# A softmax's reciprocal as a power on GpSimd, and its maximum on VectorE, in a two-layer encoder on one core

## Chip, cores, metric

One core of one Trainium2 chip. The metric is device time in microseconds of one execution of the whole program, median of the runs. Lower is better.

## What is computed

An encoder of two layers on 512 tokens of width 1024, all in float32. The first layer's attention has two groups of eight heads (grouped-query with normalised, rotated queries and keys; and latent attention with a shared rotary key). The second layer's is a neighbourhood attention of 16 heads. Each layer ends in a squared-ReLU MLP, and a last RMSNorm follows. Cut to what the change touches:

```python
def block_attention(q, k, v, scale):          # first layer, 16 heads
    sc = jnp.einsum('bkgqd,bksd->bkgqs', qblk, kt).astype(jnp.float32) * scale
    p = jax.nn.softmax(sc, axis=-1).astype(vt.dtype)
    return jnp.einsum('bkgqs,bksd->bkgqd', p, vt)

def neighbourhood_attention(h, w_qkv, rpb, w_out):   # second layer, 16 heads
    sc = jnp.einsum('bhqd,bhqkd->bhqk', qblk, kg).astype(jnp.float32) * scale + bias[None]
    p = jax.nn.softmax(sc, axis=-1).astype(vg.dtype)
    return jnp.einsum('bhqk,bhqkd->bhqd', p, vg)
```

A softmax row is exp(x - max), divided by its own sum. The division is done as a multiplication by the reciprocal of the sum.

## The kernel before

Every matmul operand is split into a high and a low part (two float32r tiles), and a product takes three matmuls: high by high, high by low, low by high. TensorE (PE) does these and all transposes. ScalarE (ACT) rounds the high parts, makes exponentials and copies PSUM banks out; VectorE (DVE) subtracts to get the low parts, adds results, and does row statistics; GpSimd (POOL) does some additions and subtractions of weights and the multiplications by the reciprocals. SyncE (SP) issues nearly all DMAs.

**First attention** (`attend`, lines 958 to 1029). The 16 heads are taken one after the other, each in four blocks of 128 queries, so there are 64 score tiles of 128x512. `scores` makes one: two or three matmuls (L997) into one of two PSUM banks `s`; a custom DVE instruction (L1001) that scales the scores by a negative number from the table `scA` or `scB`, writes them to a tile `p` in SBUF and leaves each row's minimum in `t[:, 1:2]`; ACT's exponential of minus that tile with the minimum as its bias (L1003), which leaves the row sum in `t[:, 2:3]`; DVE's reciprocal (L1004); POOL's multiplication of the 128x512 tile by it (L1005). Three blocks later, `transpose` turns the tile by four PE transposes (L972) into a bank `t`, ACT and DVE split it (L974, L975), and after every second block `values` multiplies by the head's values (L985, eight matmuls) and `fold` adds the parts (L946, L949). Between blocks PE is given other matmuls, "fill": the projections that later heads need and the first half of the output projection (L501 to L503, L907 to L909), 1.5 us by the kernel's own account after each block. There are two banks each of `s` and `t`, three of `mm`, one of `o`, and five tiles `p`. The order of instructions on each engine is here not the code's: a scheduler of the framework sets it when the program is built. On POOL stand also, in this stage, rotary multiplications (L562, L563), sums of squares (L705) and low parts of weights (L202).

**Second attention** (`attend_C`, lines 1409 to 1530). Here the code's order is kept on PE, ACT, DVE and POOL (`fixed_order`). A head has four units of 128 queries by 256 keys. `scores` makes two units (L1426) and their minimum with the bias added (L1441); `weigh` makes the exponentials (L1460); `norm` the reciprocal on DVE (L1429) and the multiplication on POOL (L1430); `turn` transposes the previous head's units (L1452). So a product of `norm` is read a head later.

**The MLPs** take most of the rest. Their weights are summed on POOL (L302 to L304), then split by ACT and DVE (L308, L309); the change does not touch them.

Of the kernel before, what the change touches and what calls it, by code (L numbers as in the profile page):

```python
# [8 lines left out]
F32 = mybir.dt.float32  # L9
F32R = mybir.dt.float32r  # L10
I32 = mybir.dt.int32
AF = mybir.ActivationFunctionType
ALU = mybir.AluOpType
AX = mybir.AxisListType
PSUM = bass.MemoryType.PSUM

S = 512
D = 1024
P = 128
# [11 lines left out]
def f32(ap):  # L31
    return ap.bitcast(F32)
# [3 lines left out]
def encoder_kernel(ctx: ExitStack, tc: tile.TileContext, ins, out, dbg=None):  # L36
    nc = tc.nc
    PE, ACT, DVE, POOL, SP = nc.tensor, nc.scalar, nc.vector, nc.gpsimd, nc.sync
# [22 lines left out]
    def nm(s):  # L61
        cnt[0] += 1
        return f"{s}_{cnt[0]}"
# [18 lines left out]
    def sbk():  # L82
        return bank("s", 2)

    def stb():
        return bank("t", 2)

    def ob():
        return bank("o", 1)
# [4 lines left out]
    def tiny(n, dt=F32):  # L94
        return tp.tile([P, n], dt, tag=f"ti{n}", name=nm("ti"))

    def keep(shape, dt, name):
        return big.tile(shape, dt, tag=name, name=name)
# [8 lines left out]
    POOL.memset(ones, 1.0)  # L107
    zeros = keep([P, 1], F32, "zeros")
    POOL.memset(zeros, 0.0)
    gs = Slot(F32)  # L110
    ACT.dma_start(cst, ins["cst"][:, 0:C_ROPE])
    ACT.dma_start(gs.t[0:16, 0:P], ins["norm_mix"].rearrange("l (k p) -> (l k) p", p=P))
# [358 lines left out]
    class Fill:  # L471
# [8 lines left out]
        def step(self):  # L480
            try:
                self.credit -= next(self.q[0][1])
            except StopIteration:
                self.q.pop(0)
# [42 lines left out]
    def bcast_cols(col_ap, nparts, bk):  # L527

        for i in range(4):
            PE.transpose(bk[0:nparts, i * P : (i + 1) * P], col_ap(i), ident)  # L530
# [38 lines left out]
    def stats_to_tok(bk, n, name):  # L569

        st = scratch()
        ACT.activation(st[0:n, :], bk[0:n, :], AF.Copy)
        tb = stb()
        for i in range(4):
            PE.transpose(tb[:, i * n : (i + 1) * n], st[0:n, i * P : (i + 1) * P], ident[0:n, 0:n])
        v = keep([P, 4 * n], F32, name)
        v3 = v.rearrange("p (i n) -> p i n", i=4)
        DVE.tensor_tensor(v3, tb[:, 0 : 4 * n].rearrange("p (i n) -> p i n", i=4),
                          r0sq.unsqueeze(2).to_broadcast([P, 4, n]), op=ALU.mult)
        DVE.tensor_scalar(v, v, 1.0, EPS, op0=ALU.mult, op1=ALU.add)  # L580
        y = rsqrt(v, 4 * n)
        DVE.tensor_tensor(v3, y.rearrange("p (i n) -> p i n", i=4),
                          r0.unsqueeze(2).to_broadcast([P, 4, n]), op=ALU.mult)
        return v3
# [17 lines left out]
    def ind2(t):  # L602
        return cst[:, C_I2 + 2 * t : C_I2 + 2 * t + 2]
# [103 lines left out]
    def q_scales():  # L707
        rs = stats_to_tok(hold["stq"], 8, "rsQ")
        sc = keep([P, 4, 8], F32, "scA")
        DVE.tensor_scalar(sc, rs, -0.125, 1.0, op0=ALU.mult, op1=ALU.mult)  # L710
        hold["scA"] = sc


# [93 lines left out]
    def latents():  # L807

        b = stb()
        for z in range(2):  # L810
            PE.matmul(b[0:2, :], ind2(z), sqs[z].t[:, 0:512], start=z == 0, stop=z == 1)
        sB = stats_to_tok(b, 2, "rsB")
        for z in range(2):
            sqs[z].free()
        scB = keep([P, 4], F32, "scB")
        DVE.tensor_scalar(scB, sB[:, :, 0], -(96.0 ** -0.5), 1.0, op0=ALU.mult, op1=ALU.mult)
        bk = stb()
        bcast_cols(lambda i: sB[:, i, 1:2].to_broadcast([P, P]), P, bk)
        hold["skvb"] = Slot(F32)
        ACT.activation(hold["skvb"].t[:, 0:512], bk, AF.Copy)  # L820
        hold["sB"], hold["scB"] = sB, scB
        for s_ in X:
            s_.free()
        yield 1.5
# [136 lines left out]
    def attend(heads, step):  # L961


        late_t, late_v = [], []

        def transpose(h, i, p):
            if i % 2 == 0:
                h["pt"] = Slot(), Slot()
            h3, l3 = (s_.t.rearrange("p (k q) -> p k q", k=4)[:, :, (i % 2) * P : (i % 2 + 1) * P] for s_ in h["pt"])
            tb = stb()  # L970
            for k in range(4):
                PE.transpose(tb[:, k * P : (k + 1) * P], p[:, k * P : (k + 1) * P], ident)  # L972
            t3 = tb.rearrange("p (k q) -> p k q", k=4)
            ACT.activation(h3, t3, AF.Copy)  # L974
            DVE.tensor_tensor(l3, t3, f32(h3), op=ALU.subtract)  # L975
            if i % 2:
                late_v.append((h, i // 2, h["pt"]))

        def values(h, half, pt):
            if half == 0:  # L980
                h["o"] = ob()
            o = h["o"]
            for k in range(4):
                for n, m in enumerate(pt):
                    PE.matmul(o[:, 256 * half : 256 * half + 256], h["vlhs"](k), m.t[:, 256 * k : 256 * k + 256],  # L985
                              start=k == 0 and n == 0, stop=k == 3 and n == 1, skip_group_check=True)
            for s_ in pt:
                s_.free()
            if half:
                fold(o, h["e"])  # L990
                h["after"]()

        def scores(h, i):
            s = sbk()
            pl = h["passes"](i)
            for n, (lh, rh) in enumerate(pl):
                PE.matmul(s, lh, rh, start=n == 0, stop=n == len(pl) - 1)  # L997
            h["done"](i)
            t = tiny(4)
            p = pp.tile([P, 512], F32, tag="p", name=nm("p"))  # L1000
            DVE.tensor_tensor_reduce(p, s, zeros.to_broadcast([P, S]), op0=ALU.add, op1=ALU.min, scale=h["scale"](i),  # L1001
                                     scalar=3e38, accum_out=t[:, 1:2])
            ACT.activation(p, p, AF.Exp, bias=t[:, 1:2], scale=-1.0, accum_out=t[:, 2:3])  # L1003
            DVE.reciprocal(t[:, 3:4], t[:, 2:3])  # L1004
            POOL.tensor_scalar(p, p, t[:, 3:4], 1.0, op0=ALU.mult, op1=ALU.mult)  # L1005
            return p

        for h in heads:
            for i in range(4):
                ripe = list(late_v)  # L1010
                p = scores(h, i)
                if len(late_t) == 3:
                    transpose(*late_t.pop(0))
                late_t.append((h, i, p))
                if ripe:
                    values(*late_v.pop(0))
                step(h, i)
        for x in late_t:
            transpose(*x)
            while late_v:  # L1020
                values(*late_v.pop(0))
            fill.run(1.5)
# [389 lines left out]
    def attend_C(step):  # L1412
# [13 lines left out]
                PE.matmul(s, lh, rh[n], start=first and n == 0, stop=n == 1, skip_group_check=True)  # L1426

        def norm(p, tt):
            DVE.reciprocal(tt[:, 2:3], tt[:, 1:2])  # L1429
            POOL.tensor_scalar(p, p, tt[:, 2:3], 1.0, op0=ALU.mult, op1=ALU.mult)  # L1430

        def scores(h, us):
# [63 lines left out]
        for n in range(16):  # L1496
            t, e = n // 2, n % 2
# [4 lines left out]
            h = dict(d=PC[t], e=e, n=n)  # L1502
# [226 lines left out]
```

## Time and profile before

| | |
|---|---|
| runs, us | 1185.4, 1184.7, 1183.35; median 1184.7 |
| span of the profiled execution, first to last instruction | 1184.0 us |
| mean granted TensorE clock | 0.994 |
| PE busy | 1160.5 us, 98% |
| DVE, ACT, POOL busy | 883.2, 640.3, 526.1 us |
| first exponential of the first attention starts | 74.6 us |
| last one | 243.1 us |
| second attention, first and last multiplication on POOL | 641.8 and 808.1 us |

The page gives the profiled execution's span and no other time for it; it is 0.7 us under the median of the runs. Times in the trace count from the span's start. In a row of instructions the first two numbers are start and length in us; in brackets stands how long the engine sat idle before it and what released it. In a group's row, "x64 | 46.2, 724 | 92.3" means 64 instructions, 46.2 us busy in all, 724 ns mean, and 92.3 us of idle time of that engine just ahead of them. A row of waits reads "engine, tile and line, <- who was waited for: us in total, times, longest". Ends of matmuls are modelled and overlap, so PE's pace is read from start to start.

### The profile page before, as it was taken

To read this page: it belongs to the slowest core of one execution; us is meant where nothing else is said; L and a number is where in the kernel's file an instruction comes from. 1 tells how busy PE (TensorE), PEld (TensorE's weight loads), DVE (VectorE), ACT (ScalarE), POOL (GpSimd) and SP (SyncE) were. 2 spreads that over 40 slices of the span, in tenths; PEclk is the share of its full clock that TensorE was granted. 3 is DMA by queue.
4 is the path that set the end of the run, shared out by engine and by line. 5 is a ranking of instruction groups with operands and counts; after the bars stand their busy time and mean duration, and the time that the engine had idled before them with its cause. 6 is when DMAs were issued, how large, how long until landed. Compare 5 with 4: busy or idle time off the path is not lost.

```text
span 1184.0 us, 19784 instructions
## 1 busy us (share of the span) xinstructions
PE 1160.5 (98%) x7128; PEld 1021.2 (86%) x7128; DVE 883.2 (75%) x1514; ACT 640.3 (54%) x1081; POOL 526.1 (44%) x662
## 2 busy tenths in 40 slices
PE   9989999999999999999999999999999999999997
PEld 8667778888899899988998998988889989998895
DVE  5788998878967368786884676667996736778975
ACT  4468676664546247562553565555554624666344
POOL 3267343224562377819602232231376625774710
PEclk9999999999999999999999999999999999999998
DMA  7223225212524723225226464433352341322412
GB/s 244 71 54 92 68 78 134 62 56 77 167 86 134 263 70 90 72 90 165 67 72 178 131 184 126 116 112 109 107 165 76 115 134 55 98 64 89 143 36 71
DMA packets 110145, 128.01 MB, mean 108 GB/s; under 512 B 9075, under 2 KB 86816, under 8 KB 110048
## 3 DMA queue, kind: packets, MB, share of 16 engines
q1 hardware_dynamic: 106992, 119.30, 33.5%
q0 software_dynamic: 2304, 6.31, 2.2%
q8 instruction: 56, 0.92, 0.3%
q10 hardware_dynamic: 752, 1.15, 0.3%
q14 instruction: 41, 0.34, 0.1%
HBM read 104.32 MB, written 6.29 MB: 93 GB/s over the span
## 4 chain that ended last, share of the span: by engine, by line
PE 81%; DVE 4%; ACT 1%; issue 1%; POOL 0%; DVEq 0%; ACTq 0%
PE mm L503 8%; PE mm L501 8%; PE mm L502 8%; PE mm L390 4%; PE mm L389 4%; PE mm L388 4%; PE t L388 3%; PE t L389 3%; PE t L390 3%; PE s L502 2%; PE s L503 2%; PE s L501 2%; PE s L390 2%; PE s L388 2%; PE s L389 2%; PE s L997 2%
## 5 line engine op out<-in xcount | busy, mean ns | idle before, releaser
L309 DVE TENSOR_TENSOR wlo<-a,whi 128x896 fp32r<-128x896 f32 x132 | 161.8, 1230 | 83.7 <-ACT whi L308 82.9
L308 ACT ACTIVATE whi<-a 128x896 fp32r<-128x896 f32 x132 | 125.0, 950 | 155.0 <-PE o L502 45.8
L501 PE MATMUL mm<-a,whi 128*128 128x512 f32 x485 | 195.9, 406 | 0.9 <-DVE a L915 0.7
L503 PE MATMUL mm<-a,wlo 128*128 128x512 f32 x485 | 192.1, 397 | 2.5 <-DVE wlo L202 2.5
L502 PE MATMUL mm<-a,whi 128*128 128x512 f32 x485 | 192.5, 397 | 0.1
L202 DVE TENSOR_TENSOR wlo<-raw,whi 128x1024 fp32r<-128x1024 f32 (+4 forms) x117 | 139.3, 1193 | 66.4 <-ACT whi L212 63.9
L212 ACT ACTIVATE whi<-raw 128x1024 fp32r<-128x1024 f32 (+3 forms) x120 | 116.4, 971 | 92.2 <-PE s L502 39.8
L302 POOL TENSOR_TENSOR a<-a 128x128 f32<-128x128 f32 x132 | 85.1, 645 | 173.3 <-DMA a<-in_ffn_w_up_dram 103.9
L303 POOL TENSOR_TENSOR a<-a 128x256 f32<-128x256 f32 x132 | 120.2, 910 | 10.3
L304 POOL TENSOR_TENSOR a<-a 128x128 f32<-128x128 f32 x132 | 115.1, 872 | 10.3
L503 PEld LDWEIGHTS mm<-a,wlo 128*128 128x128 f32 x485 | 91.7, 189 | 23.7 <-DVE wlo L202 3.4
L501 PEld LDWEIGHTS mm<-a,whi 128*128 128x128 f32 x485 | 91.8, 189 | 20.4 <-PE t L972 0.9
L502 PEld LDWEIGHTS mm<-a,whi 128*128 128x128 f32 x485 | 91.9, 190 | 17.4 <-DVE a L545 0.4
L388 PE MATMUL mm<-a,whi 128*128 128x256 f32 x370 | 103.9, 281 | 0.0
L389 PE MATMUL mm<-a,whi 128*128 128x256 f32 x370 | 103.9, 281 | 0.0
L390 PE MATMUL mm<-a,wlo 128*128 128x256 f32 x370 | 103.7, 280 | 0.0
L1005 POOL TENSOR_SCALAR p<-p,ti 128x512 f32<-128x512 f32 x64 | 46.2, 724 | 92.3 <-DVE ti L1004 81.1
L1430 POOL TENSOR_SCALAR p<-p,ti 128x256 f32<-128x256 f32 x64 | 35.6, 567 | 104.8 <-DVE ti L1429 91.8
L388 PE MATMUL t<-a,whi 128*128 128x256 f32 x264 | 74.2, 281 | 0.0
L389 PE MATMUL t<-a,whi 128*128 128x256 f32 x264 | 74.1, 281 | 0.0
L390 PE MATMUL t<-a,wlo 128*128 128x256 f32 x264 | 73.9, 280 | 0.0
L390 PEld LDWEIGHTS mm<-a,wlo 128*128 128x128 f32 x370 | 69.6, 188 | 0.2 <-DVE wlo L309 0.2
(338 smaller groups left out, 3210.8 us busy)
## 6 DMA issues: line engine op xcount, KB each, us to landing
a<-in_ffn_w_up_dram SPq DMA_DIRECT2D x104, 256.0 KB
raw<-in_ffn_w_down_dram SPq DMA_DIRECT2D x46, 512.0 KB
raw<-in_od_w_qkv_dram SPq DMA_DIRECT2D x64, 128.0 KB
a<-in_ffn_w_down_dram SPq DMA_DIRECT2D x28, 256.0 KB
raw<-in_ffn_w_up_dram SPq DMA_DIRECT2D x12, 512.0 KB
raw<-in_ev_w_in_dram SPq DMA_DIRECT2D x12, 384.0 KB
a<-a SPq DMA_DIRECT2D x18, 256.0 KB
bias<-bx SPq DMA_DIRECT2D x16, 256.0 KB
```

Source lines behind the costliest of these rows:

```text
L202: z = lambda: (eng or DVE).tensor_tensor(to, src, f32(high), op=ALU.subtract)
L212: ACT.activation(hi[:, 0:m], raw[:, 0:m], AF.Copy)
L303: POOL.tensor_tensor(r[:, 4:6], r[:, 2:3].to_broadcast([P, 2, P]), r[:, 0:7:6], op=ALU.add)
L304: POOL.tensor_tensor(r[:, 7], r[:, 3], r[:, 5], op=ALU.subtract)
L308: ACT.activation(hi[:, 0:896], raw[:, 128:1024], AF.Copy)
L309: DVE.tensor_tensor(lo[:, 0:896], raw[:, 128:1024], f32(hi[:, 0:896]), op=ALU.subtract)
L388: PE.matmul(o, wh, x[:, 0], start=kp == 0 and n in (0, 1, 3, 5), stop=False, skip_group_check=True)
L389: PE.matmul(o, wh, x[:, 1], start=False, stop=False, skip_group_check=True)
L390: PE.matmul(o, wl, x[:, 0], start=False, stop=kp == self.np - 1, skip_group_check=True)
L501: PE.matmul(o, wh, xh, start=first, stop=False)
L502: PE.matmul(o, wh, xl, start=False, stop=False)
L503: PE.matmul(o, wl, xh, start=False, stop=last)
```

## The change

In the first attention DVE now takes the row's maximum straight from the score bank and writes no tile. POOL multiplies the maximum by the scale and by -1. ACT reads the scores from the bank, scales them (the tables `scA` and `scB` become positive), adds the bias, and writes the tile `p`. POOL raises the row sum to the power -1, with a constant column `minus`, ahead of its multiplication. In the second attention only the reciprocal is replaced in the same way. After the first hunk all line numbers are higher by two: L1004 of the new kernel is the scaling, L1006 the power, L1007 the multiplication, L999 the scores, L974 the transposes, L987 the values, L503 to L505 the fill.

```diff
@@ -107,6 +107,8 @@
     zeros = keep([P, 1], F32, "zeros")
     POOL.memset(zeros, 0.0)
+    minus = keep([P, 1], F32, "minus")
+    POOL.memset(minus, -1.0)
@@ -707,7 +709,7 @@
-        DVE.tensor_scalar(sc, rs, -0.125, 1.0, op0=ALU.mult, op1=ALU.mult)
+        DVE.tensor_scalar(sc, rs, 0.125, 1.0, op0=ALU.mult, op1=ALU.mult)
@@ -813,7 +815,7 @@
-        DVE.tensor_scalar(scB, sB[:, :, 0], -(96.0 ** -0.5), 1.0, op0=ALU.mult, op1=ALU.mult)
+        DVE.tensor_scalar(scB, sB[:, :, 0], 96.0 ** -0.5, 1.0, op0=ALU.mult, op1=ALU.mult)
@@ -998,10 +1000,10 @@
             h["done"](i)
             t = tiny(4)
             p = pp.tile([P, 512], F32, tag="p", name=nm("p"))
-            DVE.tensor_tensor_reduce(p, s, zeros.to_broadcast([P, S]), op0=ALU.add, op1=ALU.min, scale=h["scale"](i),
-                                     scalar=3e38, accum_out=t[:, 1:2])
-            ACT.activation(p, p, AF.Exp, bias=t[:, 1:2], scale=-1.0, accum_out=t[:, 2:3])
-            DVE.reciprocal(t[:, 3:4], t[:, 2:3])
+            DVE.tensor_reduce(t[:, 0:1], s, axis=AX.X, op=ALU.max)
+            POOL.tensor_scalar(t[:, 1:2], t[:, 0:1], h["scale"](i), -1.0, op0=ALU.mult, op1=ALU.mult)
+            ACT.activation(p, s, AF.Exp, bias=t[:, 1:2], scale=h["scale"](i), accum_out=t[:, 2:3])
+            POOL.tensor_tensor(t[:, 3:4], t[:, 2:3], minus, op=ALU.pow)
             POOL.tensor_scalar(p, p, t[:, 3:4], 1.0, op0=ALU.mult, op1=ALU.mult)
             return p
@@ -1426,7 +1428,7 @@
         def norm(p, tt):
-            DVE.reciprocal(tt[:, 2:3], tt[:, 1:2])
+            POOL.tensor_tensor(tt[:, 2:3], tt[:, 1:2], minus, op=ALU.pow)
             POOL.tensor_scalar(p, p, tt[:, 2:3], 1.0, op0=ALU.mult, op1=ALU.mult)
```

Since the scheduler orders the first attention, the change moves more than it edits. POOL, at the start of the second group of eight heads, before (`ti` is the small tile `t` of the code, `p` the 128x512 tile; the numbers tell tiles apart, and the first of the two is the same in both kernels):

```order
L1005 TENSOR_SCALAR p_409_1788<-p_409_1788,ti_408_1787 128x512
L1005 TENSOR_SCALAR p_413_1805<-p_413_1805,ti_412_1804 128x512
L1005 TENSOR_SCALAR p_420_1833<-p_420_1833,ti_419_1832 128x512
L202 TENSOR_TENSOR wlo_444_1902<-raw_435_1885,whi_443_1901 128x2x256
L202 TENSOR_TENSOR wlo_444_1902<-raw_435_1885,whi_443_1901 128x2x128
L1005 TENSOR_SCALAR p_424_1850<-p_424_1850,ti_423_1849 128x512
```

The same engine and place in the changed kernel:

```order
L1004 TENSOR_SCALAR ti_408_1821<-ti_408_1821,scB_1415 128x1
L1004 TENSOR_SCALAR ti_412_1839<-ti_412_1839,scB_1415 128x1
L1006 TENSOR_TENSOR ti_408_1821<-ti_408_1821,minus_82 128x1
L1007 TENSOR_SCALAR p_409_1822<-p_409_1822,ti_408_1821 128x512
L1006 TENSOR_TENSOR ti_412_1839<-ti_412_1839,minus_82 128x1
L1007 TENSOR_SCALAR p_413_1840<-p_413_1840,ti_412_1839 128x512
L1004 TENSOR_SCALAR ti_419_1868<-ti_419_1868,scB_1415 128x1
L1006 TENSOR_TENSOR ti_419_1868<-ti_419_1868,minus_82 128x1
L1007 TENSOR_SCALAR p_420_1869<-p_420_1869,ti_419_1868 128x512
L1004 TENSOR_SCALAR ti_423_1886<-ti_423_1886,scB_1415 128x1
L1006 TENSOR_TENSOR ti_423_1886<-ti_423_1886,minus_82 128x1
L1007 TENSOR_SCALAR p_424_1887<-p_424_1887,ti_423_1886 128x512
```

One row a tile became three, and but for a few pairs as the first one here the scaling of a tile stands behind the multiplication of the tile ahead of it; that goes on so through the stage, with the other POOL work of the stage between.

TensorE at the score tile that comes right after these four (number 36 of 64, counted from 0), before (`s` the score banks, `t` the transposes, `mm` the fill's banks):

```order
L997 MATMUL s_445_1916<-a_368_1605,a_350_1529 128x512 x3
L972 MATMUL t_448_1926<-cst_75,p_413_1805 128x128 x4
L501 MATMUL mm_430_1878<-a_293_1302,whi_439_1893 128x512
L502 MATMUL mm_430_1878<-a_293_1302,whi_439_1893 128x512
L503 MATMUL mm_430_1878<-a_293_1302,wlo_440_1894 128x512
L501 MATMUL mm_431_1879<-a_293_1302,whi_439_1893 128x512
L502 MATMUL mm_431_1879<-a_293_1302,whi_439_1893 128x512
L503 MATMUL mm_431_1879<-a_293_1302,wlo_440_1894 128x512
L997 MATMUL s_449_1939<-a_368_1605,a_350_1529 128x512 x3
L972 MATMUL t_454_1951<-cst_75,p_420_1833 128x128 x4
```

The same tiles in the changed kernel:

```order
L999 MATMUL s_445_1954<-a_368_1634,a_350_1556 128x512 x3
L974 MATMUL t_448_1965<-cst_75,p_413_1840 128x128 x4
L999 MATMUL s_449_1978<-a_368_1634,a_350_1556 128x512 x3
L974 MATMUL t_454_1991<-cst_75,p_420_1869 128x128 x4
L987 MATMUL o_455_1998<-a_425_1893,a_381_1689 128x256
L999 MATMUL s_459_2021<-a_368_1634,a_350_1556 128x512 x2
```

The six fill matmuls that stood between these two score tiles stand further ahead now; over the stage the number of PE's matmuls is the same, but their order is not. In the second attention the engines' places stay: the power takes POOL's place just ahead of the multiplication.

## The prediction

> **What bounds the kernel now.** The page comes first: its head and shares say which engine fills the span.
>
> ```profile
> span 1184.0 us, 19784 instructions
> PE 1160.5 (98%) x7128; PEld 1021.2 (86%) x7128; DVE 883.2 (75%) x1514; ACT 640.3 (54%) x1081; POOL 526.1 (44%) x662
> ```
>
> TensorE is the bound: 23.5 us of the span are not its work, so whatever leaves VectorE can bring no more than that. The busy table by stretches shows how much of it lies in the two attentions. The first two rows are the first attention from its first to its last score tile and the second attention whole; the other five cut the first one at five of its 64 score tiles (numbered 0 to 63 in the order in which PE makes them: 0, 24, 40, 48, 52, 57, 63). Columns are the length, the busy time of each engine, the clock, DMA.
>
> ```profile
> 68.95:240.94 171.99, 165.79 (x951) 135.66 (x951) 150.44 (x357) 125.55 (x267) 74.01 (x87) 0.99 0.31 84
> 630.00:820.00 190.00, 189.36 (x1150) 166.65 (x1150) 124.28 (x335) 102.10 (x241) 53.31 (x97) 1.00 0.50 140
> 68.95:128.87 59.92, 56.07 (x297) 42.88 (x298) 51.72 (x130) 44.36 (x96) 38.12 (x41) 0.97 0.28 77
> 128.87:175.07 46.20, 44.07 (x274) 37.43 (x273) 41.94 (x104) 35.70 (x77) 16.83 (x23) 1.00 0.32 81
> 175.07:206.72 31.65, 31.43 (x189) 26.89 (x187) 27.12 (x58) 21.08 (x44) 10.04 (x12) 1.00 0.47 122
> 206.72:213.55 6.83, 6.83 (x38) 5.59 (x36) 5.12 (x15) 5.10 (x12) 2.02 (x3) 1.00 0.05 17
> 228.83:240.08 11.25, 11.25 (x73) 9.47 (x72) 10.70 (x27) 9.14 (x19) 3.48 (x5) 1.00 0.31 95
> ```
>
> The first attention holds 6.2 us without PE work (171.99 - 165.79), the second 0.6. That is all a lighter VectorE can win. What ends PE's waits there, and who waits for GpSimd now:
>
> ```profile
> PE s L997 <- DVE ti L1001: 2.9, 2, 2.4
> PEld t L972 <- POOL p L1005: 1.3, 4, 0.5
> PE t L972 <- DVE ti L1004: 0.5, 2, 0.3
> ```
>
> GpSimd stands behind TensorE with only 1.3 us of waits: today it is a follower with plenty of room.
>
> **The new chain, first attention.** Before, a tile went PE, DVE (minimum), ACT (exponential), DVE (reciprocal), POOL (multiplication), and no step of tile n+1 needed POOL to have finished tile n. In the new order (shown above) POOL stands twice in each tile, and its row that scales the maximum of tile n+1 comes behind the multiplication of tile n. POOL works in order, ACT's exponential needs the scaled maximum, and POOL's power needs that exponential. So the tiles form one serial chain, whose step R I add up from rows of today: a tile's vector work, then the shapes of POOL's operations.
>
> ```profile
> 126.95 0.07 DVE L1001 DVE_READ_ACCUMULATOR2_ANT ti<- 128x1 f32 x1
> 127.11 0.72 ACT L1003 ACTIVATE p<-p,ti 128x512 f32<-128x512 f32 x1 [0.17 <-DVE ti L1001]
> 127.74 0.19 ACT L1003 ACTIVATION_READ_ACCUMULATOR p<-p,ti 128x1 f32 x1
> 127.96 0.17 DVE L1004 RECIPROCAL ti<-ti 128x1 f32<-128x1 f32 x1
> 128.30 0.69 POOL L1005 TENSOR_SCALAR p<-p,ti 128x512 f32<-128x512 f32 x1 [4.06 <-DVE ti L166]
> ...
> L1005 POOL TENSOR_SCALAR p<-p,ti x64: 688/696/1653, 77.6 to 244.3; 128x512 f32<-128x512 f32 x64
> L1430 POOL TENSOR_SCALAR p<-p,ti x64: 471/482/1697, 641.8 to 808.1; 128x256 f32<-128x256 f32 x64
> L109 POOL MEMSET zeros<- 128x1 f32 x1 | 0.1, 99 | 0.0
> L202 POOL TENSOR_TENSOR wlo<-raw,whi 128x128 fp32r<-128x128 f32 x2 | 0.9, 468 | 0.0
> L202 POOL TENSOR_TENSOR wlo<-raw,whi 128x512 fp32r<-128x512 f32 x10 | 14.5, 1451 | 5.2 <-ACT whi L222 4.1 <-ACT whi L212 1.1
> L303 POOL TENSOR_TENSOR a<-a 128x256 f32<-128x256 f32 x132 | 120.2, 910 | 10.3
> ```
>
> - POOL's scaling, 128x1: the same kind of instruction takes 0.696 us at 512 columns and 0.482 at 256, so 0.214 per 256 and about 0.27 at one column.
> - POOL to ACT: no row; DVE to ACT is 0.09 (127.02 to 127.11), I take 0.10.
> - Exponential with its row sum: 127.11 to 127.93, 0.82.
> - ACT to POOL: nearest is DVE to POOL, 128.13 to 128.30, 0.17.
> - The power, 128x1: no row shows one. From below, the cheapest one-column operation of POOL, 0.10; from above, its two-input operation on 512 columns, 1.45. I take **0.47**, the smallest two-input row, because a power is more work an element than a subtraction and 128 columns are more elements than one.
> - The multiplication waits for the power of its own engine: L303 also waits for POOL's row before it, 10.3 us / 132 = 0.08.
> - The multiplication, 0.70.
>
> R = 0.27 + 0.10 + 0.82 + 0.17 + 0.47 + 0.08 + 0.70 = **2.61 us** a tile. The reciprocal that leaves DVE (0.16) was no step of any such chain. The minimum that becomes a maximum stays one pass over 512 columns and lies ahead of the chain: I count it at nothing, hidden by the previous tile's 2.61; uncovered it would be some 0.1 either way a tile.
>
> GpSimd Engine Reference of the Trainium skill, section 4.1, speaks against the change: it sends elementwise work to VectorE and calls GpSimd about twice as slow on two inputs. By that ratio and the 0.16 us reciprocal the power would be an estimated 0.32, and the sum below some 5 us smaller; no run here shows a power on it yet.
>
> **Where the chain shows on TensorE.** There are two score banks, and each is now read until its exponential ends. So PE can lead by two tiles, and where PE has less than R of work a tile, it waits. What its rows cost, start to start:
>
> ```profile
> 163.11 0.86 PE L997 MATMUL s<-a,a 96*128 96x512 f32 x3
> 163.80 0.60 PE L972 MATMUL t<-cst,p 128*128 128x128 f32 x4
> 164.16 0.47 PE L501 MATMUL mm<-a,whi 128*128 128x512 f32 x1
> ...
> 165.63 0.86 PE L997 MATMUL s<-a,a 96*128 96x512 f32 x3
> 166.32 0.60 PE L972 MATMUL t<-cst,p 128*128 128x128 f32 x4
> 166.68 1.19 PE L985 MATMUL o<-a,a 128*128 128x256 f32 x8
> 167.71 0.39 PE L501 MATMUL mm<-a,whi 128*128 128x512 f32 x1
> 167.94 0.39 PE L502 MATMUL mm<-a,whi 128*128 128x512 f32 x1
> ```
>
> Three scores 0.69, four transposes 0.36, eight values 1.03, a projection matmul 0.23. With these prices I count the new order of PE between score tiles. It is uneven: the projections stand in heaps, and between the heaps come runs of tiles with next to none.
>
> - Tiles 0 to 23. PE alone: 7.0 us in tiles 0 and 1, 10.2 in 21 to 23. In 2 to 20 PE has 31.5 us of work, the chain 19 x 2.61 = 49.6. Three pairs of tiles stand as scale, scale, power, multiply, power, multiply, which saves 1.1 each: -3.3. POOL's rotary, square and weight-split rows that stand between a multiplication and the next scaling (0.47 to 1.45 each by the L202 rows) add 9.2. So 55.5. Half a step (1.3) is forgiven for PE's lead. 7.0 + 55.5 + 10.2 - 1.3 = 71.4 against 59.9: **+11.5**.
> - Tiles 24 to 39: 24 (7.1), 27 to 31 (17.8) and 38, 39 (5.3) are PE's; 25, 26 and 32 to 37 are the chain's, 8 x 2.61 = 20.9 where PE has 10.7. 51.1 - 2.6 for two leads = 48.5 against 46.2: **+2.3**.
> - Tiles 40 to 47: PE's rows are the same and above R on average (31.65 / 8 = 4.0): 0.
> - Tiles 48 to 51: three chain steps and 2.7 of PE, 10.5 - 1.3 = 9.2 against 6.83: **+2.4**.
> - Tiles 57 to 62: six chain steps, 15.7 - 1.3 = 14.4 against 11.25: **+3.1**.
>
> Sum **+19.3 us**. Today's own waits are inside the measured lengths that I compare with, so they are not counted again.
>
> **Second attention.** The order keeps its places: each reciprocal becomes a POOL row just ahead of its multiplication, 64 times 0.47 + 0.08 = 35 us on POOL, which is busy 53.3 of 190. PE reads a head's products one head later, and a head lasts (808.1 - 641.8) / 16 = 10.4 us, in which POOL gets four more rows, 2.2 us. I cost it at 0; TensorE's 98% and that lead hide it. If the lead were gone, the price would be those 35 us, four at a time. The 64 reciprocals off DVE win nothing, with PE busy 189.36 of 190. The new constant is one 0.10 us memset while PE waits for its first loads.
>
> The profiled span, 1184.0, lies 0.7 below the median of the runs, 1184.7; nothing outside the span changes, so 1184.7 + 19.3 = **1204 us**.
>
> **Rivals.**
> - *The chain is shorter than PE's own pace (not slower).* The chain decides in 36 tiles (19 + 8 + 3 + 6), so 19.3 / 36 = 0.54 less a step, R = 2.07, brings the sum to zero: both small POOL steps at the memset's 0.10. Below that the second part of today's DVE waits goes (2.9 + 0.5 us above) and the time is about 1181. For it: one-column operations may be that cheap. Against: both read a scalar from memory, and one is a power. 17 in 100.
> - *The power is dear.* At 1.45 us, R = 3.59 and the sum is 19.3 + 36 x 0.98 = 54.6; at 1.0 it is 38.4, so 1223. From 1.1 on the time is over 1227. For it: nothing here computes a function on POOL. 20 in 100, half of that over 1239.
> - *The clock falls.* Today PE's longest wait there is followed by slow matmuls:
>
> ```profile
> 74.61 0.76 PE L997 MATMUL s<-a,a 128*128 128x512 f32 x2 [2.39 <-DVE ti L1001]
> 75.00:79.00 4.00, 4.00 (x12) 3.10 (x11) 2.39 (x8) 2.74 (x8) 0.69 (x1) 0.57 0.00 0
> ```
>
> After 2.39 us of waiting the granted clock is 0.57 for 4 us, 1.7 us lost. My waits are about R less a sparse tile, 2.61 - 0.8 = 1.8 at most; if one in four of the 36 tiles drops the clock, that is 9 x 1.7 = 15 more, 1219. TensorE: Matmul & The Clock Gate of the Trainium skill, "What's actually happening", puts the halving after an idle window of about 3.4 us; by it waits of 1.8 us would leave the clock alone and the sum as it is, but the trace fell after a single wait of 2.39. 13 in 100.
>
> The forecast itself, with a power from 0.2 to 1.1 us and the clock up: 50 in 100.
>
> **Numbers.** A power of 0.10 with the scaling as taken gives 19.3 - 13.3 = 6, so 1191; with the scaling at 0.10 too it is 1185. The upper end is 1239 plus a little clock. The range 1184 to 1242 leaves out the faster case (about 12) and a power beyond 1.5 (about 7). A measurement here tells apart 0.2%, 2.4 us: faster 0.12, within that 0.05, slower 0.83.
>
> **What would show it.** In the new profile: POOL's power row with its mean; POOL's idle time ahead of it ended by ACT's exponential and ACT's idle ahead of the exponential ended by POOL's scaling; PE's scores waiting for ACT, a new line among its waits, of 15 to 30 us in all; the first attention some 191 us instead of 172, the second still 99% PE. Steps between multiplications in tiles 32 to 37 of 2.6 us confirm R. I am wrong if the scores wait as little as now, if the second attention's PE falls under 185 of 190, or if the power is outside 0.1 to 1.45.

## The result, and the profile after

The changed kernel takes 1224.8 us (median of 4 runs, 1224.45 to 1225.52) against 1184.7 for the kernel before on the same chip: 40.0 us more, a ratio of 1.0342 with a 95% interval of 1.0328 to 1.0356. The forecast was 1204.0, so the direction and the mechanism came as written, inside the range, but the loss is twice the 19.3 us of the sum.

The page's head and shares of the changed kernel answer to the two lines that opened the prediction.

```profile
span 1222.7 us, 19841 instructions
PE 1170.8 (96%) x7128; PEld 1023.5 (84%) x7128; DVE 869.5 (71%) x1322; ACT 644.5 (53%) x1081; POOL 635.2 (52%) x855
```

VectorE lost only 14 us of work, GpSimd gained 109, and TensorE now stands still for 51.9 us where it did for 23.5. No engine but TensorE is above three quarters, so no second engine became full: of the 38.7 us that the span grew, 28.4 are TensorE waiting.

The busy table by stretches says where (columns as in the prediction: window, length, then PE, PEld, DVE, ACT, POOL, then clock and DMA). First the first attention from its first to its last score tile, then the second attention whole, then the stretches of tiles 0 to 23, 24 to 39, 40 to 47, 57 to 62.

```profile
68.22:279.60 211.38, 177.80 (x951) 139.78 (x952) 143.32 (x235) 129.08 (x267) 130.41 (x211) 0.97 0.25 68
...
665.00:855.00 190.00, 189.68 (x1147) 166.65 (x1145) 120.99 (x273) 102.66 (x240) 100.75 (x160) 1.00 0.52 140
...
68.22:145.19 76.97, 61.29 (x297) 45.03 (x298) 48.38 (x78) 46.14 (x95) 57.56 (x87) 0.93 0.22 60
145.19:201.40 56.21, 47.79 (x274) 37.47 (x273) 39.78 (x74) 35.33 (x75) 30.30 (x53) 1.00 0.26 66
201.40:237.77 36.37, 31.51 (x188) 26.91 (x187) 26.56 (x43) 23.08 (x48) 20.79 (x32) 1.00 0.41 109
262.11:279.60 17.49, 14.42 (x76) 11.68 (x75) 13.60 (x19) 10.41 (x22) 9.16 (x17) 0.90 0.20 61
```

The whole loss lies in the first attention: 211.38 - 171.99 = 39.4 us. The second attention's TensorE is busy 189.68 of 190 as before, though GpSimd's work there has nearly doubled (53.31 to 100.75). In the first, TensorE's idle time rose from 6.2 to 33.6 us (+27.4), and its busy time from 165.79 to 177.80 (+12.0) for the same 951 matmuls. Part of those 12 us is the clock (0.97 against 0.99), and part is that the profile books a matmul which starts after a wait at its whole length, while matmuls in a row overlap; the two are not told apart.

What ends TensorE's waits in the whole program, the four longest rows (us in total, times, longest), and then the two longest rows among all engines in the window of the first attention:

```profile
PE s L999 <- ACT p L1005: 15.9, 21, 2.3
PE o L987 <- DVE a L977: 5.7, 4, 2.7
PE o L987 <- DVE sc L951: 3.6, 4, 1.0
PE t L974 <- POOL p L1007: 3.4, 5, 1.0
```

```profile
ACT p L1005 <- POOL ti L1004: 69.2, 55, 3.0
POOL ti L1006 <- ACT p L1005: 48.8, 46, 7.1
```

The last two rows are the chain, seen from both of its ends: the exponential waits for GpSimd's scaling 55 times of 64, and GpSimd's power waits for the exponential 46 times of 64. TensorE's first row is where that reaches the bound: a score tile needs a bank that an exponential has not yet left. GpSimd's own rows in tiles 32 to 36 show one turn after another:

```profile
189.21 0.27 POOL L1004 TENSOR_SCALAR ti<-ti,scB 128x1 f32<-128x1 f32 x1
190.47 0.55 POOL L1006 TENSOR_TENSOR ti<-ti,minus 128x1 f32<-128x1 f32 x1 [0.98 <-ACT p L1005]
191.11 0.69 POOL L1007 TENSOR_SCALAR p<-p,ti 128x512 f32<-128x512 f32 x1
191.78 0.27 POOL L1004 TENSOR_SCALAR ti<-ti,scB 128x1 f32<-128x1 f32 x1
193.03 0.55 POOL L1006 TENSOR_TENSOR ti<-ti,minus 128x1 f32<-128x1 f32 x1 [0.98 <-ACT p L1005]
193.68 0.69 POOL L1007 TENSOR_SCALAR p<-p,ti 128x512 f32<-128x512 f32 x1
194.34 0.27 POOL L1004 TENSOR_SCALAR ti<-ti,scB 128x1 f32<-128x1 f32 x1
...
189.52 0.78 ACT L1005 ACTIVATE p<-s,ti,scB 128x512 f32<-128x512 f32 x1 [1.76 <-POOL ti L1004]
```

From scaling to scaling it is 2.57 us, twice the same to 0.01. The parts: scaling to exponential 189.21 to 189.52, 0.31; exponential to power 0.95; power to multiplication 0.64; multiplication to the next scaling 0.67.

### The profile page after: what moved, and what is told of

Same layout as the page of the kernel before. It is cut to its first block, busy times and chain, and to the rows that moved or that the text cites. A ratio compares the mean times of both kernels' runs of the same rounds, so it can differ in the third digit from the quotient of the medians.

```text
span 1222.7 us, 19841 instructions
## 1 busy us (share of the span) xinstructions
PE 1170.8 (96%) x7128; PEld 1023.5 (84%) x7128; DVE 869.5 (71%) x1322; ACT 644.5 (53%) x1081; POOL 635.2 (52%) x855
## 4 chain that ended last, share of the span: by engine, by line
PE 79%; POOL 7%; DVE 7%; ACT 4%; issue 3%; POOLq 0%; DVEq 0%; ACTq 0%
PE mm L503 7%; PE mm L504 7%; PE mm L505 7%; PE mm L392 3%; PE mm L391 3%; PE mm L390 3%; PE t L390 3%; PE t L391 3%; PE t L392 3%; PE s L505 2%; PE s L504 2%; PE s L503 2%; POOL p L1007 2%; PE s L392 2%; PE s L390 2%
## 5 line engine op out<-in xcount | busy, mean ns | idle before, releaser
L503 PE MATMUL mm<-a,whi 128*128 128x512 f32 x485 | 195.8, 405 | 3.4 <-DVE a L510 2.0
L505 PE MATMUL mm<-a,wlo 128*128 128x512 f32 x485 | 191.4, 395 | 2.2 <-DVE wlo L204 2.2
L204 DVE TENSOR_TENSOR wlo<-raw,whi 128x1024 fp32r<-128x1024 f32 (+4 forms) x117 | 139.6, 1195 | 71.1 <-ACT whi L214 70.8
L304 POOL TENSOR_TENSOR a<-a 128x128 f32<-128x128 f32 x132 | 85.6, 648 | 165.7 <-DMA a<-in_ffn_w_up_dram 103.0
L306 POOL TENSOR_TENSOR a<-a 128x128 f32<-128x128 f32 x132 | 119.3, 904 | 10.4
L503 PEld LDWEIGHTS mm<-a,whi 128*128 128x128 f32 x485 | 91.3, 188 | 23.7 <-DVE a L510 2.8
L505 PEld LDWEIGHTS mm<-a,wlo 128*128 128x128 f32 x485 | 91.2, 188 | 23.2 <-DVE wlo L204 3.0
L504 PEld LDWEIGHTS mm<-a,whi 128*128 128x128 f32 x485 | 91.6, 189 | 17.8 <-DVE a L832 0.8
L1431 POOL TENSOR_TENSOR ti<-ti,minus 128x1 f32<-128x1 f32 x64 | 49.4, 772 | 54.7 <-ACT p L1462 51.2
L999 PE MATMUL s<-a,a 96*128 96x512 f32 (+1 forms) x160 | 53.3, 430 | 17.3 <-ACT p L1005 15.9
```

The lines of the kernel that those rows point to most:

```text
L204: z = lambda: (eng or DVE).tensor_tensor(to, src, f32(high), op=ALU.subtract)
L306: POOL.tensor_tensor(r[:, 7], r[:, 3], r[:, 5], op=ALU.subtract)
L503: PE.matmul(o, wh, xh, start=first, stop=False)
L504: PE.matmul(o, wh, xl, start=False, stop=False)
L505: PE.matmul(o, wl, xh, start=False, stop=last)
```

## Experiments

The question is not only whether the chain exists but why it costs 40 us and not 19. At first three explanations stood beside each other. The first is the chain: GpSimd's scaling of a tile stands behind the power and multiplication of the tile ahead. The rivals need no chain: GpSimd's new work as such (a dear power, longer transfers of a result to the next engine), or the new order of TensorE's rows. The measured times are given as medians and as differences to the median of the kernel before on the same chip (1183.9 or 1184.0).

Most measurements below use the starts of the scores of tiles 0, 24, 40, 48, 52, 57 and 63 in each trace; the lengths between them, in us:

| kernel | 0-23 | 24-39 | 40-47 | 48-51 | 52-56 | 57-62 | sum |
|---|---|---|---|---|---|---|---|
| before | 59.9 | 46.2 | 31.6 | 6.8 | 15.3 | 11.3 | 171.1 |
| after | 77.0 | 56.2 | 36.4 | 7.9 | 16.4 | 17.3 | 211.2 |
| e1, division a tile later | 68.3 | 51.3 | 33.3 | 7.9 | 15.2 | 12.9 | 188.9 |
| e2, scaling on VectorE | 67.9 | 45.5 | 32.3 | 7.1 | 15.3 | 14.7 | 182.8 |
| e3, only the power | 62.5 | 44.8 | 31.6 | 7.2 | 15.2 | 11.2 | 172.6 |
| e4, multiplication for power | 71.4 | 52.8 | 34.1 | 7.6 | 15.2 | 15.0 | 196.0 |
| e5, reciprocal on VectorE | 66.3 | 51.5 | 34.3 | 7.2 | 15.9 | 15.5 | 190.6 |
| e6, neither on GpSimd | 65.4 | 46.4 | 31.5 | 7.1 | 15.3 | 14.0 | 179.7 |
| e7, three powers | 103.6 | 70.8 | 49.1 | 10.2 | 21.8 | 22.6 | 278.1 |
| e9, one more VectorE row | 61.9 | 48.0 | 31.5 | 7.3 | 15.2 | 11.7 | 175.6 |
| e10, exponential from the bank | 64.5 | 45.9 | 31.6 | 7.2 | 15.3 | 12.0 | 176.5 |

Two things blur this table by a few us. In e2 and e6 ten more of TensorE's matmuls stand between the first and the last score (961 against 951, some 2 us that the rest of the program has less). And the granted clock differs from trace to trace: over the stage it was 0.97 after, 1.00 in e1, 0.98 in e4 and 0.85 in e7, against 0.99 before.

**Break the chain, keep every operation.** Power and multiplication of a tile are issued behind the scaling of the next tile, so that a scaling no longer stands behind a power that waits for the exponential just ahead (shortened; `divide` issues the two removed POOL lines).

```diff
-            POOL.tensor_scalar(t[:, 1:2], t[:, 0:1], h["scale"](i), -1.0, ...)
+            sc = POOL.tensor_scalar(t[:, 1:2], t[:, 0:1], h["scale"](i), -1.0, ...)
             ACT.activation(p, s, AF.Exp, bias=t[:, 1:2], scale=h["scale"](i), accum_out=t[:, 2:3])
-            POOL.tensor_tensor(t[:, 3:4], t[:, 2:3], minus, op=ALU.pow)
-            POOL.tensor_scalar(p, p, t[:, 3:4], 1.0, op0=ALU.mult, op1=ALU.mult)
+            late_n.append((t, p))
+            if len(late_n) == 2:
+                divide(sc)      # power and multiplication of the tile ahead, placed behind sc
```

Expected:

> All operations of the changed kernel, but each power and its multiplication are issued one score tile later, behind the next tile's scaling on GpSimd; TensorE's order stays nearly row for row. Theory 1 (serial chain: a tile's scaling stands behind the previous tile's power and multiplication, so each exponential, and all that ScalarE has behind it, waits): the chain is cut, 1186 to 1200 us. Theory 2 (it is the 64 powers of 0.55 us themselves): nothing is taken away, 1215 or more. Theory 3 (the scheduler's more uneven order of TensorE): the order is kept, 1215 or more.

Measured: 1202.5 us, +18.6, ratio 1.0152 (1.0133 to 1.0172). More than half of the loss, 21 us, is gone with the same operations on the same engines and TensorE's rows almost in the same order (96% of its rows in the stage stand in the same sequence). So neither the new work of GpSimd as such nor the order makes that half. A part of the 21 us is the clock, which fell in the changed kernel and not in e1: at most 6.3 us, by the sum at the end of the next section. GpSimd's rows show the chain open: the scaling now waits for the maximum, and the power waits for nothing.

```profile
187.84 0.27 POOL L1004 TENSOR_SCALAR ti<-ti,scB 128x1 f32<-128x1 f32 x1 [0.62 <-DVE ti L1003]
188.06 0.55 POOL L1013 TENSOR_TENSOR ti<-ti,minus 128x1 f32<-128x1 f32 x1
188.71 0.69 POOL L1017 TENSOR_SCALAR p<-p,ti 128x512 f32<-128x512 f32 x1
190.62 0.27 POOL L1004 TENSOR_SCALAR ti<-ti,scB 128x1 f32<-128x1 f32 x1 [1.21 <-DVE ti L1003]
```

But it stays 2.5 us above the range that the chain alone would allow: 18.6 us are left. Some of that is e1's own, since a product that comes a tile later also reaches its transposes later (they wait 5.2 us for it, against 3.4 in the changed kernel). The next runs take the parts one by one.

**One part at a time.** Four runs fill a square: scaling on GpSimd or VectorE, division on GpSimd or VectorE. In e2 the scaling goes to VectorE:

```diff
-            POOL.tensor_scalar(t[:, 1:2], t[:, 0:1], h["scale"](i), -1.0, op0=ALU.mult, op1=ALU.mult)
+            DVE.tensor_scalar(t[:, 1:2], t[:, 0:1], h["scale"](i), -1.0, op0=ALU.mult, op1=ALU.mult)
```

> The changed kernel with the maximum scaled on VectorE instead of GpSimd; power and multiplication stay on GpSimd. Theory 1: no GpSimd step ahead of an exponential, no chain, 1184 to 1194 us. Theory 2 (the powers themselves): 1205 to 1225. Theory 3 (order): the scheduler orders anew, between the two kernels in likeness, so anything from 1190 to 1220.

In e5 the first attention's reciprocal goes back to VectorE:

```diff
-            POOL.tensor_tensor(t[:, 3:4], t[:, 2:3], minus, op=ALU.pow)
+            DVE.reciprocal(t[:, 3:4], t[:, 2:3])
```

> The changed kernel with the first attention's power put back as VectorE's reciprocal; scaling and multiplication stay on GpSimd, so the serial chain stays, with a shorter step: 2.57 less power and its wait (0.65) plus the hop over VectorE (0.19), about 2.11 us. Rule P (the loss is the plain sum of step less TensorE's own work, over the tiles where the step is longer; today's other waits come on top): 25 us, so 1209. Rule Q (as predicted: the chain takes the place of today's waits and TensorE's lead is forgiven): 5 to 8 us, about 1191. If the power itself were the matter and not the chain: 1184 to 1190.

In e6 both edits are made, and the second attention has its VectorE reciprocal too; what is left of the change is the maximum without a copy of the tile, its scaling as a row of its own on VectorE, and the exponential that reads the bank.

> The changed kernel with nothing moved to GpSimd: maximum, scaling and reciprocal all on VectorE in both attentions, the exponential still read from the score bank. If GpSimd's part (chain, power, late products) is the whole loss: 1183 to 1187. If reading the scores from the bank until the exponential ends, or the reordering, costs by itself what the run with the scaling on VectorE still lost (11): 1190 to 1196.

Measured, as us over the kernel before (ratio and interval below it):

| | division on VectorE | division on GpSimd |
|---|---|---|
| scaling on VectorE | e6: +7.8, 1.0068 (1.0053 to 1.0082) | e2: +11.5, 1.0096 (1.0080 to 1.0112) |
| scaling on GpSimd | e5: +20.1, 1.0172 (1.0158 to 1.0187) | after: +40.0, 1.0342 (1.0328 to 1.0356) |

The power alone costs 3.7 us, the scaling alone 12.3, both together 32.2. The power alone makes the products late: TensorE's transposes wait 5.4 us for them in e2 and 2.0 in e6. The scaling alone already closes a chain, with a shorter step, since it stands behind the multiplication of the tile ahead, which waits for VectorE's reciprocal. In e5 the scaling ahead of these two rows starts at 179.46, so the step is 2.20 us:

```profile
180.99 0.70 POOL L1007 TENSOR_SCALAR p<-p,ti 128x512 f32<-128x512 f32 x1 [1.26 <-DVE ti L1006]
181.66 0.70 POOL L1004 TENSOR_SCALAR ti<-ti,scB 128x1 f32<-128x1 f32 x1
```

So the 16 us beyond the sum of the two fit what the power costs inside that chain, where it lengthens the step from 2.20 to 2.57 us; e4 below shortens it by 0.36 us in the same order and gives back 13.5. The order plays no large part between e5 and the changed kernel (95% of TensorE's rows in the stage in the same sequence); for e2 and e6 (80 and 74%) this table cannot tell it apart. And 7.8 us come from neither scaling nor power (e6 is in the upper of its two expected ranges): that is a part of the change which the prediction counted at nothing. e2, at 1195.4, lies 1.5 us above what was expected of it with the chain as the only cause. e5, at 1204.1, lies nearer to the 1209 of the plain sum explained below than to the other times expected of it.

**The power alone in the kernel before.** In e3 only the reciprocal of the first attention is a power on GpSimd, and the minimum is taken as before.

```diff
-            DVE.reciprocal(t[:, 3:4], t[:, 2:3])
+            POOL.tensor_tensor(t[:, 3:4], t[:, 2:3], minus, op=ALU.pow)
```

> The kernel before, with nothing changed but the reciprocal of the first attention, which becomes a power on GpSimd ahead of its multiplication. Theory 1: GpSimd stands behind the exponential only, 1183 to 1188 us. Theory 2: the 64 powers are there, 1205 to 1225. Theory 3: TensorE's order is close to that of before, 1183 to 1190.

Measured: 1187.4 us (7 runs), +3.5, ratio 1.0027 (1.0015 to 1.0039). The same 64 powers that cost 20 us in the changed kernel (40.0 - 20.1) cost 3.5 where GpSimd has no other step of the next tile behind them. The price of an operation is here set by what stands behind it in its queue.

**The length of the step.** Two kernels change R and leave the rest. In e4 the power is a multiplication in the same place (the result is then no softmax); all of TensorE's rows stand in the order of the changed kernel, one for one.

```diff
-            POOL.tensor_tensor(t[:, 3:4], t[:, 2:3], minus, op=ALU.pow)
+            POOL.tensor_tensor(t[:, 3:4], t[:, 2:3], minus, op=ALU.mult)
```

> The changed kernel, row for row in the same order on TensorE, ScalarE and GpSimd, with the power of the first attention replaced by a multiplication of the same shape by the same column (the rows are then scaled by minus their sum, not divided by it). Theory 1: the step shortens by the difference of the two operations, for which I guess 0.2 to 0.3 us, in 36 to 64 tiles: 7 to 19 us less, 1206 to 1218. Theory 2: the same sum over 64 tiles, 1206 to 1212. Theory 3: no difference, 1222 to 1227.

In e7 there are three powers, one behind the other (the second and third undo and redo the first); here 93% of TensorE's rows in the stage keep their sequence:

```diff
             POOL.tensor_tensor(t[:, 3:4], t[:, 2:3], minus, op=ALU.pow)
+            POOL.tensor_tensor(t[:, 3:4], t[:, 3:4], minus, op=ALU.pow)
+            POOL.tensor_tensor(t[:, 3:4], t[:, 3:4], minus, op=ALU.pow)
```

> The changed kernel with three powers in a row in the first attention instead of one (the result is the same reciprocal): the step grows by 2 x (0.55 + 0.10) to 3.87 us, 56 of 63 tiles then have less work on TensorE than that. Rule P: 104 us, so about 1288. Rule Q: 16 of today's waits and some 8 of leads off, about 1264. If the power were hidden: no change from 1224.

Measured: e4 1210.4 us, +26.5, ratio 1.0225 (1.0207 to 1.0242); e7 1295.0 us, +111.0, ratio 1.0941 (1.0924 to 1.0959). The steps, scaling to scaling, first in e4 (2.21 us) and then in e7 (3.83 us):

```profile
181.97 0.26 POOL L1004 TENSOR_SCALAR ti<-ti,scB 128x1 f32<-128x1 f32 x1
183.22 0.19 POOL L1006 TENSOR_TENSOR ti<-ti,minus 128x1 f32<-128x1 f32 x1 [0.99 <-ACT p L1005]
183.51 0.70 POOL L1007 TENSOR_SCALAR p<-p,ti 128x512 f32<-128x512 f32 x1
184.18 0.27 POOL L1004 TENSOR_SCALAR ti<-ti,scB 128x1 f32<-128x1 f32 x1
```

```profile
240.94 0.27 POOL L1004 TENSOR_SCALAR ti<-ti,scB 128x1 f32<-128x1 f32 x1
242.19 0.55 POOL L1006 TENSOR_TENSOR ti<-ti,minus 128x1 f32<-128x1 f32 x1 [0.98 <-ACT p L1005]
242.82 0.55 POOL L1007 TENSOR_TENSOR ti<-ti,minus 128x1 f32<-128x1 f32 x1
243.45 0.55 POOL L1008 TENSOR_TENSOR ti<-ti,minus 128x1 f32<-128x1 f32 x1
244.09 0.70 POOL L1009 TENSOR_SCALAR p<-p,ti 128x512 f32<-128x512 f32 x1
244.77 0.27 POOL L1004 TENSOR_SCALAR ti<-ti,scB 128x1 f32<-128x1 f32 x1
```

These two decide how the chain is to be summed. For each of the 63 steps between two score tiles I add TensorE's rows at the prediction's prices and take what is missing to R, with nothing taken off; that is the plain sum.

| kernel | step R, us | plain sum of R less rows | stage less 171.1, measured |
|---|---|---|---|
| e4 | 2.21 | 28.8 | +24.9 |
| after | 2.57 | 40.9 | +40.1 |
| e7 | 3.83 | 102 | +107.0 |

A step shorter by 0.36 us gave back 13.5 us (40.0 - 26.5) in a kernel with all rows in the same places: the chain sets the pace in about 38 tiles, and 40 steps have less than 2.57 us of rows. e4 by itself also fits the rival of the powers as such (1206 to 1212 expected); e1 and e3 are what speaks against that. For e7 the plain sum had 1288 on record and the sum made as in the prediction 1264; it measured 1295. The clock is in these stages too, in e7 above all (0.85), and the plain sum has no term for it. For e5 the plain sum is too high: with a step of 2.20 us it gives about 28, and the stage grew by 19.5. The order of TensorE's rows is no cause by this reckoning: with the rows in the order of the kernel before, the plain sum at 2.57 is 40.6, the same.

**The second attention alone.** In e8 the change is made only there.

```diff
         def norm(p, tt):
-            DVE.reciprocal(tt[:, 2:3], tt[:, 1:2])
+            POOL.tensor_tensor(tt[:, 2:3], tt[:, 1:2], minus, op=ALU.pow)
```

> The kernel before with the power in the second attention alone; TensorE's and ScalarE's order is that of before, row for row. As predicted: hidden, 1182.5 to 1186. If GpSimd's later products hold up the transposes or the score tiles: 1187 to 1195.

Measured: 1183.9 us (11 runs), ratio 1.0001 (0.9992 to 1.0010). GpSimd does 50 us of powers more, and TensorE's stretch does not change:

```profile
L1431 POOL TENSOR_TENSOR ti<-ti,minus 128x1 f32<-128x1 f32 x64 | 50.0, 781 | 54.3 <-ACT p L1462 54.2
...
630.00:820.00 190.00, 189.43 (x1150) 166.66 (x1149) 121.24 (x274) 104.31 (x244) 100.56 (x159) 1.00 0.51 138
```

**The 7.8 us without GpSimd.** Two candidates in e6: the exponential starts a VectorE row later, or the score bank is held until the exponential ends. In e9 the kernel before gets one more one-column VectorE row between minimum and exponential:

```diff
+            DVE.tensor_scalar(t[:, 1:2], t[:, 0:1], 1.0, 1.0, op0=ALU.mult, op1=ALU.mult)
             ACT.activation(p, p, AF.Exp, bias=t[:, 1:2], scale=-1.0, accum_out=t[:, 2:3])
```

> The kernel before, with one more one-column VectorE instruction between the minimum and the exponential (a multiplication by 1), so that the exponential starts later by about the 0.2 us of such a row and its semaphore; the tile is still written to SBUF by the minimum's instruction and the bank is free when that ends. The version with nothing of the stage on GpSimd but the multiplication cost +7.9 us. If that is the extra VectorE row and the reordering that any new row brings: +5 to +9 here. If it is the bank that is held until the exponential ends: +0 to +2 here. The order of PE's rows is as like that of the kernel before (0.97) as that of the version it stands for (0.96).

In e10 the exponential of the kernel before reads the bank, with a second table of positive scales:

```diff
-            ACT.activation(p, p, AF.Exp, bias=t[:, 1:2], scale=-1.0, accum_out=t[:, 2:3])
+            ACT.activation(p, s, AF.Exp, bias=t[:, 1:2], scale=h["pos"](i), accum_out=t[:, 2:3])
```

> The kernel before, with the exponential reading the score bank (scaled by a second, positive table, two small VectorE rows in the whole program) and not the tile in SBUF, so that the bank is held until the exponential ends and the exponential takes the 0.78 us of a bank instead of 0.72; no row is added a tile and nothing moves to GpSimd. If the held bank is what the version without GpSimd paid for: +5 to +9. If it was the extra VectorE row: +0 to +2. If both cases come out at +3 to +5, the two share it; if both come out under +2, the maximum's own instruction and the order are left.

Measured: e9 1188.9 us, +4.9, ratio 1.0043 (1.0030 to 1.0056); e10 1193.0 us, +9.0, ratio 1.0074 (1.0062 to 1.0087). Neither is nothing, and together they exceed the 7.8 us that they should explain. TensorE's waits of e10 do not settle it; the two longest rows, and that of the exponential:

```profile
PE mm L501 <- DVE a L508: 2.5, 1, 2.5
PE mm L503 <- DVE wlo L202: 2.0, 2, 1.8
...
PE s L1003 <- ACT p L1009: 1.4, 3, 0.8
```

The scores wait 1.4 us for the bank that the exponential holds; in the kernel before they wait 2.9 us for the minimum, so TensorE's waits for the banks did not grow. The longest are waits of projections, 1.8 of the 2.0 us in the second row outside this stage. The scheduler put each of these kernels in another order: of TensorE's rows in the stage 74% (e9) and 84% (e10) keep the sequence of the kernel before, in e6 65%. So two kernels with the bank read by the exponential take 8 and 9 us more, but how much of it is the held bank and how much the order that came with the edit stays open.

## Why the prediction was wrong in size

**Step R: right.** 2.61 us predicted, 2.57 measured. Scaling with the way to ACT 0.37 against 0.31; exponential with the way back 0.99 against 0.95; power with the wait for itself 0.55 against 0.64; multiplication 0.70 against 0.67. The disputed power took 0.55 us against 0.47:

```profile
L1006 POOL TENSOR_TENSOR ti<-ti,minus x64: 543/550/1125, 76.6 to 284.6; 128x1 f32<-128x1 f32 x64
L1431 POOL TENSOR_TENSOR ti<-ti,minus x64: 542/552/1639, 681.8 to 849.6; 128x1 f32<-128x1 f32 x64
L1004 POOL TENSOR_SCALAR ti<-ti,scB x32: 254/267/1229, 185.3 to 283.4; 128x1 f32<-128x1 f32 x32
L1005 ACT ACTIVATE p<-s,ti,scB x32: 767/778/783, 185.6 to 283.7; 128x512 f32<-128x512 f32 x32
```

(The three numbers with slashes are the shortest, the median and the longest of a group, in ns.) The estimate of 0.32 us by GPSIMD Engine Reference of the Trainium skill, section 4.1, does not hold: 0.55 against VectorE's 0.16 is 3.4 times, not twice, and the measurement decides.

**Where it shows: right.** The scores wait for the exponential 15.9 us, inside the 15 to 30 named; ACT and GpSimd wait for each other as named. **The second attention at nothing: right** (e8). **Rivals:** the power was not dear and the chain not shorter.

**The sum: wrong, and this is the step that failed.** The prediction set its chain stretches against the measured lengths of the kernel before and wrote: "Today's own waits are inside the measured lengths that I compare with, so they are not counted again." It also forgave half a step at each stretch, for TensorE's lead. Without these two its terms give 55.5 - 31.5 = 24.0 in tiles 2 to 20, 51.1 - (7.1 + 17.8 + 5.3 + 10.7) = 10.2 in 24 to 39; by the same prices 3.9 in 48 to 51 and 4.7 in 57 to 62. That is 42.8 (with +9.2 and -3.3 for GpSimd's other rows and the pairs, which the plain sum by tile leaves out); 40.1 was measured. What took it down to 19.3 were 6.5 us of leads (five halves of 1.3) and some 17 us by which the kernel before is slower than its rows: 11.2 in tiles 0 to 23, where the rows come to 7.0 + 31.5 + 10.2 = 48.7 and 59.9 were measured, and 5.3 in 24 to 39. The prediction let the chain swallow that difference, as if the old waits stood in the tiles where the chain waits. By stretches, in us over the kernel before:

| tiles | predicted | plain sum by tile, about | measured |
|---|---|---|---|
| 0-23 | +11.5 | +23 | +17.1 |
| 24-39 | +2.3 | +10 | +10.0 |
| 40-47 | 0 | 0 | +4.7 |
| 48-51 | +2.4 | +4 | +1.1 |
| 52-56 | 0 | 0 | +1.2 |
| 57-62 | +3.1 | +4 | +6.1 |

In tiles 24 to 39 nothing was to be taken off: the old slack and the leads, 7.9 us in the prediction, stayed in full. In tiles 0 to 23 the chain did swallow some: beside rows and plain sum about 11 us are left before and about 5 after, so 6 of the 12.5 us taken off were rightly off. In tiles 48 to 51 the lead was worth all that was forgiven and more. Tiles 40 to 47 and 52 to 56 cost 5.9 us where the prediction had nothing, and 57 to 62 cost 3.0 more than it had. So the larger part of the error is a subtraction of time that stayed, and most of the rest lies in stretches put at nothing; old slack and leads are not told apart.

That the plain sum meets the total, 40.9 against 40.1, is in part luck: it is some 6 us too high in tiles 0 to 23 and 3 in 48 to 51, and too low by 5 in 40 to 47 and by 1 to 2 in each of the last two. e4 and e7 miss in the same places (tiles 0 to 23: 17 against 11.5 measured, and 49 against 43.7; 40 to 47: 0 against 2.5, and 5 against 17.5). The three step lengths show that the loss grows with the step as the tile by tile sum says, not that each stretch does.

**Tiles 40 to 47: also wrong.** TensorE's rows there are above R on average, and the prediction stopped at that. But GpSimd has longer rows between a multiplication and the next scaling, and an engine's rows run in their order here: whatever stands behind the waiting exponential on ACT is late too. One such place, GpSimd's, ACT's, VectorE's and TensorE's rows:

```profile
207.79 1.29 POOL L204 TENSOR_TENSOR wlo<-raw,whi 128x512 fp32r<-128x512 f32 x1
...
211.62 1.73 POOL L564 TENSOR_TENSOR sc<-sc,a 128x512 f32<-128x512 f32 x1
...
209.36 0.78 ACT L1005 ACTIVATE p<-s,ti,scB 128x512 f32<-128x512 f32 x1 [2.18 <-POOL ti L1004]
...
210.13 0.59 ACT L856 ACTIVATE sc<-mm 128x512 f32<-128x512 f32 x1
...
210.75 0.01 DVE L562 LOAD_MASK_SELECT sc<-sc  x1 [2.85 <-ACT sc L856]
...
213.38 0.69 DVE L568 TENSOR_TENSOR sc<-sc,sc 128x512 f32<-128x512 f32 x1 [0.56 <-POOL sc L564]
213.99 0.68 DVE L977 TENSOR_TENSOR a<-t,a 128x512 fp32r<-128x512 f32 x1
...
214.73 1.09 PE L987 MATMUL o<-a,a 128*128 128x256 f32 x7 [2.69 <-DVE a L977]
```

GpSimd's split of weights (1.29 us) delays the scaling and ACT idles 2.18 us ahead of the exponential. The copy behind it on ACT is late, VectorE idles 2.85 us for that copy, GpSimd's rotary multiplication (1.73 us) and VectorE's addition follow, and the split of the transposed tile, which needs none of these, stands behind them on VectorE. TensorE's values wait 2.69 us for that split. Waits of the values (5.7 + 3.6 us above) were not in the prediction at all. This is one place; how much of the 4.7 us such places make was not measured.

**The maximum and the held bank at nothing: wrong.** With nothing of the change on GpSimd (e6) it is still +7.8 us. The prediction named the bank ("each is now read until its exponential ends") and used it only for the lead. Which part of the edit, or of the new order, these us belong to is open. Nor is it shown how they enter the 40 us of the changed kernel, which the plain sum reaches without them.

**The clock: partly.** It fell three times in the stage, the third time in the last stretch (0.90 above). The other two, TensorE's row after a wait and the windows around it:

```profile
100.64 1.13 PE L999 MATMUL s<-a,a 128*128 128x512 f32 x2 [1.39 <-ACT p L1005]
...
124.20 0.86 PE L999 MATMUL s<-a,a 128*128 128x512 f32 x2 [2.34 <-ACT p L1005]
...
100.00:104.00 4.00, 3.36 (x11) 2.78 (x12) 1.71 (x3) 2.43 (x6) 2.15 (x5) 0.60 0.08 28
...
124.00:128.00 4.00, 2.80 (x9) 1.94 (x10) 1.67 (x3) 1.92 (x6) 3.36 (x7) 0.58 0.16 49
128.00:132.00 4.00, 4.00 (x20) 3.55 (x19) 2.11 (x4) 2.74 (x7) 2.28 (x5) 0.56 0.00 0
```

Busy time by what the clock lacks gives 3.36 x 0.40 + 2.80 x 0.42 + 4.00 x 0.44 = 4.3 us here. In all, the clock stood at 0.50 for 13.6 us of the stage, with TensorE busy 12.6 of them: at most 6.3 us by the same estimate, since some of that time TensorE would have waited anyway. The rival had nine drops and 15 us. TensorE: Matmul & The Clock Gate of the Trainium skill, "What's actually happening", has the clock halved after an idle window of about 3.4 us. The rows don't show an idle stretch of that length: the clock fell after waits of 1.39 and 2.34 us. In the 3.41 us ahead of the three drops TensorE was busy 1.29, 1.07 and 1.90 us, at a clock of 1.00.

## What to carry to other kernels

An in-order engine that stands twice in the life of a tile, once before and once after another engine's step, ties consecutive tiles together; look for its two rows in the order before counting what each costs, since the same powers cost 3.5 us with one such row and 20 with two. Sum such a chain tile by tile against the bound engine's own rows, and do not subtract waits that the old trace has in other tiles; expect the total to come out better than its stretches, and leave room for what stands behind the chain on the other engines. Put the second row of a tile behind the first row of the next one, as e1 did: that took back 21 of 40 us; none of the versions here beat the kernel before.

## What the runs showed of the hardware

A power of one column (128x1) on GpSimd takes 0.55 us, a multiplication of the same shape 0.19 (183/191/763 ns in e4), a scaling by a scalar from memory 0.27; some of each take 0.6 to 1.2 us, and in the second attention the power's mean is 0.77 against a median of 0.55, for which no run here names a cause. A result goes from GpSimd to ACT within 0.31 us of the start of a 0.27 us row. The exponential of a 128x512 tile takes 0.78 us from a PSUM bank and 0.72 from SBUF.
